# A two-block transformer on one core: weight splits ordered behind the layer norm at stage borders, the mean in one instruction, first loads and last columns cut differently

## The chip, the cores and the metric

The kernel runs on one core of one Trainium2 chip. The metric is the device time of one execution in microseconds (us). Runs of this kernel lie between 2589.7 and 2595.17 us, so a change of less than 0.2% (5.2 us) can hardly be told from none.

## The reference, cut to what matters

256 tokens of width 1024 pass through two blocks of two layers each, all in float32. The stages that the change touches are these:

```python
# first block, for l in 0, 1
x = layer_norm(a*x + 0.5*swiglu(x, ffn1_w1[l], ffn1_w3[l], ffn1_w2[l]), ln1_g[l], ln1_b[l])
x = layer_norm(a*x + token_mixing(x, w_in[l], ...), ln2_g[l], ln2_b[l])
x = layer_norm(a*x + cross_attention(x, mem, ...), ln3_g[l], ln3_b[l])
x = layer_norm(a*x + 0.5*swiglu(x, ffn2_w1[l], ffn2_w3[l], ffn2_w2[l]), ln4_g[l], ln4_b[l])
# second block, for l in 0, 1
x = x + 0.5*swiglu(rmsnorm(x), ...); x = x + mixer_l(rmsnorm(x)); x = x + 0.5*swiglu(rmsnorm(x), ...)
x = x + sigmoid(rmsnorm(x) @ ple_gate[l]) * (p[l] @ ple_proj[l])
return rmsnorm(x, final_norm)
```

Here `swiglu(h, w1, w3, w2) = (silu(h @ w1) * (h @ w3)) @ w2`, with w1 and w3 of 1024 x 2816 and w2 of 2816 x 1024.

## The kernel before

The 256 tokens are two tiles of 128 rows, called t = 0 and t = 1. Every matrix product takes each operand as a sum of two parts, hi + lo, and adds three matmuls (`mm3`): x_hi w_hi, x_hi w_lo and x_lo w_hi, lines 191, 192 and 193. TensorE (PE) runs these; a stationary tile is 128 x 128 of x, and up to 512 columns of w stream past it.

**Weights.** A `slot` is a piece of a weight matrix of 128 x 1024 elements (two k blocks of 512 columns, or one k block of 1024). It is loaded by SyncE (SP) into one of four `raw` buffers; then ScalarE (ACT) copies each half into `whi` (line 177) and VectorE (DVE) subtracts to get `wlo` (line 178). Eight pairs of `whi` and `wlo` exist. A raw buffer is free for the next load when its two copies and two subtractions are done; loads are issued in one order on SP's queue.

**A stage's border.** A stage ends in `lin_rows`: t = 0 finishes first, its layer norm runs beside the matmuls of t = 1, then comes t = 1. The layer norm (`layer_norm`) forms y and its row sums on DVE (`lny`, line 344), the mean in two DVE instructions (347, 348), the square sum on ACT (`lnj`, 351), 1/sigma on DVE and GpSimd (353, 354, a power), then the normalized row on DVE (358, 359). `x_to_T` turns it with eight PE transposes, and ACT and DVE split the result into `xT` (304, 305; 386, 387 where a row scale is folded in). The turn of t = 1 is put off as `pend`.

The next stage begins with `lin_first`. It runs all its weight slots (four for each of its one or two `specs`) for t = 0 alone; after a number of matmuls given by its argument `at`, `flush` issues the put-off turn of t = 1; then it runs the same slots for t = 1. So 48 matmuls on t = 0 hide the layer norm of t = 1 where there are two specs. The slots are numbered here in the order in which they are made, 0 to 7.

The order on each engine is fixed when the program is made, by a planner that takes instructions by their place in the program and by its own idea of when their inputs are ready; `issue_after(ins)` makes the planner put an instruction after `ins` if both are on the same engine, without a wait on the chip.

**The ends.** At the start x of t = 0 is loaded whole, then two slots of w1, then x of t = 1, then the two broadcast rows `G` and `B` of the first layer norm (512 KB each), then more slots. At the end the last stage (`ple_step` with no next norm) forms for each 512-column half a sigmoid, a product, a sum and a square sum, then 1/rms, then for each half one DVE instruction and one store.

Of the kernel before, what the change touches and what calls it, by code (L numbers as in the profile page):

```python
# [11 lines left out]
ALU = mybir.AluOpType  # L12
# [82 lines left out]
class Core:  # L95
    def __init__(self, tc, ctx, a):
        self.tc, self.a = tc, a
        nc = self.nc = tc.nc
        self.V, self.A, self.G, self.T = nc.vector, nc.scalar, nc.gpsimd, nc.tensor
        e = ctx.enter_context  # L100

        self.wsp = e(tc.tile_pool(name="wsp", bufs=8))
        self.xp = e(tc.tile_pool(name="xp", bufs=1))
        self.bp = e(tc.tile_pool(name="bp", bufs=11))
        self.cst = e(tc.tile_pool(name="cst", bufs=1))
        self.wraw = e(tc.tile_pool(name="wraw", bufs=4))
        self.rp = e(tc.tile_pool(name="rp", bufs=2))
        self.gbp = e(tc.tile_pool(name="gbp", bufs=1))
        self.sc2 = e(tc.tile_pool(name="sc2", bufs=7))
        self.sc4 = e(tc.tile_pool(name="sc4", bufs=2))  # L110
        self.biasp = e(tc.tile_pool(name="biasp", bufs=2))
        self.smp = e(tc.tile_pool(name="smp", bufs=5))
        self.accp = e(tc.tile_pool(name="accp", bufs=4, space=PSUM))
        self.atp = e(tc.tile_pool(name="atp", bufs=2, space=PSUM))
        self.tpp = e(tc.tile_pool(name="tpp", bufs=2, space=PSUM))
        self.pend = None
        self.ident = self.const("c_ident")
        self.mhalf = self.cst.tile([P, 32], F32, name="mhalf")
        self.V.memset(self.mhalf, -0.5)
        self.one = self.cst.tile([P, 1], F32, name="one")  # L120
        self.V.memset(self.one, 1.0)
# [97 lines left out]
    def lin_first(self, X, specs, at):  # L219


        ps = [[self.bank("lin") for _ in specs] for _ in range(2)]
        slots, i = [], 0
        for t in range(2):
            for j, (wv, c0, n, evac) in enumerate(specs):
                for b in range(4):
                    if t == 0:
                        slots.append(wv(b) if callable(wv) else self.slot_kn(wv, 2 * b, 2, c0, n))
                    wh, wl = slots[4 * j + b]
                    for k in range(2):  # L230
# [24 lines left out]
    def lin_rows(self, X, ks, wv, done, skew=6, mid=None, last=False, late=None):  # L255

        o = [[self.bank("o") for _ in range(2)] for _ in range(2)]
        ks = list(ks)  # L260
# [3 lines left out]
        def unit(w, kk, t, hs=(0, 1)):  # L264
            xh, xl = X(kk, t)
            for h in hs:
                sl = slice(h * 512, h * 512 + 512)
# [21 lines left out]
        with self.tc.issue_after(mm.ins):  # L289
            if last:  # L290
                todo = [(w, kk, (h,)) for h in range(2) for w, kk in ws]
# [46 lines left out]
    def layer_norm(self, t, x, o, c, G, B, xT):  # L338
# [8 lines left out]
        self.V.tensor_add(mu[:, 0:1], sm[:, 0:1], sm[:, 1:2])  # L347
        self.V.tensor_scalar_mul(mu[:, 1:2], mu[:, 0:1], -1.0 / D)
        var = self.sm(1, "var")
        junk = self.s4(name="lnj")  # L350
        self.A.activation(junk, y, AF.Square, bias=mu[:, 1:2], accum_out=var)
# [4 lines left out]
        for h in range(2):  # L356
            sl = slice(h * 512, h * 512 + 512)
            self.V.scalar_tensor_tensor(xn[:, sl], y[:, sl], mu[:, 1:2], G[:, sl], op0=ALU.add, op1=ALU.mult)
            self.V.scalar_tensor_tensor(xn[:, sl], xn[:, sl], rs, B[:, sl], op0=ALU.mult, op1=ALU.add)
# [46 lines left out]
    def ffn(self, xT, w1, w3, w2, done, rs=None, mid=None, pre=()):  # L406
# [18 lines left out]

        for c in range(5):
            if c == 0:
                h = [[None, None], [None, None]]

# [4 lines left out]
                yield from self.lin_first(X, [(first(w1v), 0, 512, keep(0)), (first(w3v), 0, 512, keep(1))], 36)  # L434
            else:
                h = [[self.bank("h") for _ in range(2)] for _ in range(2)]
            for i, wv in enumerate((w1v, w3v) if c else ()):
                for k0 in range(0, 8, 2):
# [5 lines left out]
                    if i == 0 and k0 == 0:  # L444
# [382 lines left out]
    def mixing(self, l, xT, done):  # L827
# [14 lines left out]
        def plain(c0, n, dst):  # L842
# [17 lines left out]
                               38))  # L860
# [654 lines left out]
def body(tc, a):  # L1515
    with ExitStack() as ctx:
# [5 lines left out]
        pre = []  # L1522
        for t in range(2):
            if t == 1:
                pre = [k.slot_kn(w1v, 2 * i, 2, 0, 512) for i in range(2)]
            x[t] = k.new_x(t)
            nc.sync.dma_start(out=x[t], in_=a["x"][0, t * P:(t + 1) * P, :])
            for h in range(2):
                tp = k.tp()
                for j in range(4):  # L1530
                    k.T.transpose(tp[:, j, :], x[t][:, (4 * h + j) * P:(4 * h + j + 1) * P], k.ident)
                k.split_to(xT[:, 4 * h:4 * h + 4, 0, t * P:(t + 1) * P],
                           xT[:, 4 * h:4 * h + 4, 1, t * P:(t + 1) * P], tp)
# [4 lines left out]
        def ln_step(g, b, c, norm=None):  # L1538

            G = k.row_bcast(g, "G")  # L1540
            B = k.row_bcast(b, "B")
            gcol = k.rows_T([rows(norm)], "gcol") if norm is not None else None
            st = {}

            def done(t, o):
                if t == 0:
                    st["T"] = k.new_xT()
                x[t], fin = k.layer_norm(t, x[t], o, c, G, B, st["T"])
# [26 lines left out]
        def ple_step(norm):  # L1575
# [5 lines left out]
            def done(t, o):  # L1581
# [5 lines left out]
                def part(h):  # L1587
                    sl = slice(h * 512, h * 512 + 512)
                    k.A.activation(s[:, sl], o[h], AF.Sigmoid, scale=rs[t])
# [3 lines left out]
                if norm is not None:  # L1593
                    for h in range(2):
                        part(h)
# [4 lines left out]
                else:  # L1600
                    ss = k.sm(2, "fss")
                    for h in range(2):
                        part(h)
                        k.mean_sq(ss[:, h:h + 1], xn[:, h * 512:h * 512 + 512], 512)
                    r = k.sm(1, "frs")
                    k.V.tensor_add(r, ss[:, 0:1], ss[:, 1:2])
                    k.V.tensor_scalar(r, r, 0.5, RMS_EPS, op0=ALU.mult, op1=ALU.add)
                    k.G.tensor_tensor(r, r, k.mhalf[:, 0:1], op=ALU.pow)
                    for h in range(2):
                        sl = slice(h * 512, h * 512 + 512)  # L1610
                        k.V.scalar_tensor_tensor(s[:, sl], xn[:, sl], r, G[:, sl], op0=ALU.mult, op1=ALU.mult)
# [5 lines left out]
        for l in range(2):  # L1617
            st, done = ln_step(a["ln1_g"][l], a["ln1_b"][l], 0.5)
            run_all(k.ffn(xT, a["ffn1_w1"][l], a["ffn1_w3"][l], a["ffn1_w2"][l], done, pre=pre,
                          mid=lambda: k.mixing_prep(l)))  # L1620
            pre = []
            xT = st["T"]
            st, done = ln_step(a["ln2_g"][l], a["ln2_b"][l], 0.5)
            memT = k.mixing(l, xT, done)
            xT = st["T"]
            st, done = ln_step(a["ln3_g"][l], a["ln3_b"][l], 1.0)
            k.xattn(l, xT, memT, done)
            xT = st["T"]
            st, done = ln_step(a["ln4_g"][l], a["ln4_b"][l], 0.5, a["ffn_norm_2"][0, 0] if l == 1 else None)
            run_all(k.ffn(xT, a["ffn2_w1"][l], a["ffn2_w3"][l], a["ffn2_w2"][l], done))  # L1630
# [53 lines left out]
```

## Time and profile before

| | us |
|---|---|
| median of 3 runs (2589.7 to 2595.17) | 2589.87 |
| the profiled execution, its own time | 2592.86 |
| its span, first to last instruction | 2590.9 |
| PE busy | 2557.8 (99%) |
| DVE busy | 1654.6 (64%) |
| ACT busy | 1405.3 (54%) |

PE, DVE, ACT, POOL and SP are TensorE, VectorE, ScalarE, GpSimd and SyncE; PEld is PE's weight load. The page gives each engine's busy time. Matmuls are pipelined, so the time from the start of one to the start of the next is less than the duration that a row shows. A view of waits names the instruction that waited, and after the arrow the engine and instruction that ended its wait. A view of stretches lists for each engine the busy time and in brackets the instructions that overlap the stretch, in the order PE, PEld, DVE, ACT, POOL.

### The profile page before, as it was taken

The numbers are of one execution on the slowest core, as the hardware profiler recorded it, in microseconds if no ns is written. First come the engines' busy times: TensorE is split into PE (matmuls) and PEld (weight loads), VectorE is DVE, ScalarE is ACT, GpSimd is POOL, SyncE is SP. The second block draws the span as 40 slices with busy tenths as digits, with TensorE's granted clock in tenths as the row PEclk, the third lists the DMA queues.
The fourth block names the chain that finished last, engine by engine and source line by source line (L and its number), as shares of the span: only waits on it lengthen the run. The fifth ranks groups of instructions, "written<-read, shape, count | busy, mean of one in ns | idle before, by whom it ended". The sixth has DMA issues, their size and how long they took to land.

```text
span 2590.9 us, 35713 instructions
## 1 busy us (share of the span) xinstructions
PE 2557.8 (99%) x12769; PEld 2136.5 (82%) x12769; DVE 1654.6 (64%) x3254; ACT 1405.3 (54%) x2804; POOL 78.1 (3%) x122
## 2 busy tenths in 40 slices
PE   8999999999999999999999999999999999999998
PEld 7888888888888889878888888887788788878887
DVE  6548687676556557687775565567655655566555
ACT  5445646555545445546555455456644645766544
POOL 0000010000000000010000000000000000000000
PEclk9999999999999999999999999999999999999999
DMA  8658655547556558564456556563665665454652
GB/s 282 189 163 229 185 163 158 162 147 219 183 177 211 189 163 228 166 177 139 156 180 201 188 180 196 188 178 111 192 188 182 194 187 194 140 171 148 195 190 98
DMA packets 261800, 465.40 MB, mean 180 GB/s; under 512 B 25963, under 2 KB 96119, under 8 KB 261623
## 3 DMA queue, kind: packets, MB, share of 16 engines
q1 hardware_dynamic: 261622, 463.13, 58.4%
q8 instruction: 100, 1.64, 0.3%
q14 instruction: 78, 0.63, 0.1%
HBM read 462.02 MB, written 1.05 MB: 179 GB/s over the span
## 4 chain that ended last, share of the span: by engine, by line
PE 91%; DVE 4%; ACT 2%; DMA 2%; issue 1%; POOL 0%; DVEq 0%; POOLq 0%; SPq 0%; ACTq 0%
PE h L193 9%; PE h L191 9%; PE h L192 9%; PE lin L193 8%; PE lin L191 8%; PE lin L192 8%; PE o L193 8%; PE o L192 8%; PE o L191 8%; PE tp L313 2%; PE linT L251 2%; PE linT L250 2%; PE linT L249 2%; DVE wlo L178 1%; PE po L542 1%; PE ht L193 1%
## 5 line engine op out<-in xcount | busy, mean ns | idle before, releaser
L178 DVE TENSOR_TENSOR wlo<-raw,whi 128x512 fp32r<-128x512 f32 (+2 forms) x1682 | 1095.3, 687 | 650.6 <-ACT whi L177 646.4
L177 ACT CAST whi<-raw 128x512 fp32r<-128x512 f32 (+2 forms) x1682 | 962.5, 615 | 813.7 <-PE h L193 313.5
L191 PE MATMUL h<-whi,xT 128*128 128x512 f32 x1024 | 401.2, 392 | 0.0
L193 PE MATMUL h<-whi,xT 128*128 128x512 f32 x1024 | 398.9, 390 | 0.0
L192 PE MATMUL h<-wlo,xT 128*128 128x512 f32 x1024 | 398.7, 389 | 0.0
L191 PE MATMUL lin<-whi,xT 128*128 128x512 f32 (+1 forms) x912 | 363.0, 400 | 4.2 <-ACT xT L386 2.1
L193 PE MATMUL lin<-whi,xT 128*128 128x512 f32 (+1 forms) x912 | 353.0, 390 | 3.2 <-DVE xT L305 3.2
L192 PE MATMUL lin<-wlo,xT 128*128 128x512 f32 (+1 forms) x912 | 353.1, 388 | 0.2 <-DVE wlo L178 0.2
L191 PE MATMUL o<-whi,gT 128*128 128x512 f32 x704 | 276.1, 392 | 0.0
L192 PE MATMUL o<-wlo,gT 128*128 128x512 f32 x704 | 274.9, 391 | 0.0
L193 PE MATMUL o<-whi,gT 128*128 128x512 f32 x704 | 274.1, 389 | 0.0
L193 PEld LDWEIGHTS h<-whi,xT 128*128 128x128 f32 x1024 | 192.2, 188 | 40.1
L192 PEld LDWEIGHTS h<-wlo,xT 128*128 128x128 f32 x1024 | 192.4, 188 | 39.1
L191 PEld LDWEIGHTS h<-whi,xT 128*128 128x128 f32 x1024 | 192.3, 188 | 38.8
L191 PEld LDWEIGHTS lin<-whi,xT 128*128 128x128 f32 x912 | 171.9, 189 | 43.9 <-ACT xT L386 6.6
L193 PEld LDWEIGHTS lin<-whi,xT 128*128 128x128 f32 x912 | 171.7, 188 | 39.8 <-DVE xT L305 4.3
L192 PEld LDWEIGHTS lin<-wlo,xT 128*128 128x128 f32 x912 | 172.2, 189 | 32.0 <-DVE wlo L178 1.0
L193 PEld LDWEIGHTS o<-whi,gT 128*128 128x128 f32 x704 | 132.2, 188 | 27.4
L191 PEld LDWEIGHTS o<-whi,gT 128*128 128x128 f32 x704 | 132.2, 188 | 26.8
L192 PEld LDWEIGHTS o<-wlo,gT 128*128 128x128 f32 x704 | 132.3, 188 | 26.3
L249 PE MATMUL linT<-xT,whi 128*128 128x256 f32 (+1 forms) x264 | 75.2, 285 | 0.0
L251 PE MATMUL linT<-xT,wlo 128*128 128x256 f32 (+1 forms) x264 | 74.9, 284 | 0.0
(474 smaller groups left out, 3163.8 us busy)
## 6 DMA issues: line engine op xcount, KB each, us to landing
raw<-in_ffn_w SPq DMA_DIRECT2D x496, 512.0 KB
raw<-in_w_in SPq DMA_DIRECT2D x120, 512.0 KB
raw<-in_m_w_in SPq DMA_DIRECT2D x52, 512.0 KB
raw<-in_ffn_w SPq DMA_DIRECT2D x64, 256.0 KB
raw<-in_w_o SPq DMA_DIRECT2D x16, 512.0 KB
raw<-in_m_w_out SPq DMA_DIRECT2D x16, 512.0 KB
raw<-in_ple_gate SPq DMA_DIRECT2D x16, 512.0 KB
bias<-in_b_in SPq DMA_DIRECT2D x24, 256.0 KB
```

The costliest lines, as they stand in the source:

```text
L177: self.A.copy(hi[:, v], raw[:, v])
L178: self.V.tensor_sub(lo[:, v], raw[:, v], hi[:, v].bitcast(F32))
L191: mm(ps, xh, wh, start=start, stop=False)
L192: mm(ps, xh, wl, start=False, stop=False)
L193: return mm(ps, xl, wh, start=False, stop=stop)
L249: mm(ps[:m, :], wh[:, k, :], xh, start=(k == 0), stop=False)
L250: mm(ps[:m, :], wh[:, k, :], xl, start=False, stop=False)
L251: mm(ps[:m, :], wl[:, k, :], xh, start=False, stop=(k == nk - 1))
L313: self.T.transpose(tp[:, j, :], src[:, (b + j) * P:(b + j + 1) * P], self.ident)
L542: self.T.matmul(po[:, j * dv:(j + 1) * dv], pT[:, j * (t + 1) + k, :], v_of(hs[j], k), start=(k == 0), stop=(k == t))
```

## The change

It has five parts.

1. `layer_norm` takes the mean in one DVE instruction instead of two and remembers three of its instructions in `heads`: the mean, the square, the last of line 359. The next `lin_first` puts slots 3 and 4 behind the square (on ACT) and the mean (on DVE), and slots 5 to 7 behind the square and the last of line 359. `heads` is that of t = 1.
2. `at` becomes 32 for the feed-forward stages (from 36) and 35 for the mixing stage (from 38).
3. At the start x of t = 0 comes in two halves with the first slot's two halves between them, x of t = 1 comes after the second slot, its turn becomes `pend`, the first `lin_first` takes w1 alone and `at` 15, and w3 follows in the ordinary loop.
4. `G` and `B` of a layer norm that ends a feed-forward stage are loaded in the middle of that stage's `lin_rows` and no longer ahead of the stage.
5. In the last stage the second half of t = 1 becomes two pieces of 256 columns; the product with the final gain moves ahead of 1/rms; the last scaling is one DVE instruction and one ACT instruction.

```diff
@@ lin_first
+        norm, self.heads = self.heads, None
+
+        def slot(wv, b, c0, n):
+            with ExitStack() as q:
+                if norm is not None and len(slots) >= 3:
+                    q.enter_context(self.tc.issue_after(norm[1].ins))
+                    q.enter_context(self.tc.issue_after(norm[2 if len(slots) >= 5 else 0].ins))
+                return wv(b) if callable(wv) else self.slot_kn(wv, 2 * b, 2, c0, n)
...
-                        slots.append(wv(b) if callable(wv) else self.slot_kn(wv, 2 * b, 2, c0, n))
+                        slots.append(slot(wv, b, c0, n))
@@ lin_rows
+        cols = [[(0, 512), (512, 512)] for _ in range(2)]
         o = [[self.bank("o") for _ in range(2)] for _ in range(2)]
+        if last:
+            cols[1][1:] = [(512, 256), (768, 256)]
+            o[1] = [o[1][0], o[1][1][:, 0:256], self.at("o")[:, 0:256]]
...
-                todo = [(w, kk, (h,)) for h in range(2) for w, kk in ws]
+                todo = [(w, kk, (h,)) for h in range(3) for w, kk in ws]
@@ layer_norm
-        self.V.tensor_add(mu[:, 0:1], sm[:, 0:1], sm[:, 1:2])
-        self.V.tensor_scalar_mul(mu[:, 1:2], mu[:, 0:1], -1.0 / D)
+        m = self.V.tensor_scalar(mu[:, 1:2], sm[:, 0:1], sm[:, 1:2], -1.0 / D, op0=ALU.add, op1=ALU.mult)
...
-        self.A.activation(junk, y, AF.Square, bias=mu[:, 1:2], accum_out=var)
+        sq = self.A.activation(junk, y, AF.Square, bias=mu[:, 1:2], accum_out=var)
...
-            self.V.scalar_tensor_tensor(xn[:, sl], xn[:, sl], rs, B[:, sl], op0=ALU.mult, op1=ALU.add)
+            v = self.V.scalar_tensor_tensor(xn[:, sl], xn[:, sl], rs, B[:, sl], op0=ALU.mult, op1=ALU.add)
+        self.heads = (m, sq, v)
@@ ffn
+        start = bool(pre)
...
-                yield from self.lin_first(X, [(first(w1v), 0, 512, keep(0)), (first(w3v), 0, 512, keep(1))], 36)
+                specs = [(first(w1v), 0, 512, keep(0)), (first(w3v), 0, 512, keep(1))]
+                yield from self.lin_first(X, specs[:1] if start else specs, 15 if start else 32)
...
-            for i, wv in enumerate((w1v, w3v) if c else ()):
+            for i, wv in enumerate((w1v, w3v)):
+                if h[0][i] is not None:
+                    continue
@@ mixing
-                               38))
+                               35))
@@ body
+        x = [k.new_x(t) for t in range(2)]
+        def load_x(t, h):
+            sl = slice(h * 512, h * 512 + 512)
+            nc.sync.dma_start(out=x[t][:, sl], in_=a["x"][0, t * P:(t + 1) * P, sl])
+
+        def first_parts(raw):
+            v = raw.rearrange("p (k n) -> p k n", n=512)
+            yield v[:, 0:1], w1v[:, 0:1, 0:512]
+            load_x(0, 1)
+            yield v[:, 1:2], w1v[:, 1:2, 0:512]
+        load_x(0, 0)
+        pre = [[w.rearrange("p (k n) -> p k n", n=512) for w in k.slot(first_parts, 1024)]]
+        k.x_to_T(0, x[0], xT)
+        pre.append(k.slot_kn(w1v, 2, 2, 0, 512))
+        for h in range(2):
+            load_x(1, h)
+        k.pend = lambda: k.x_to_T(1, x[1], xT)
@@ ple_step, no next norm
+                    for i, ps in enumerate(o):
+                        n = ps.shape[-1]
+                        part(ps, slice(c0, c0 + n))
+                        junk = k.s2(name="junk")
+                        k.A.activation(junk[:, :n], xn[:, c0:c0 + n], AF.Square, scale=512.0 ** -0.5,
+                                       accum_out=ss[:, i:i + 1])
+                        k.V.tensor_mul(s[:, c0:c0 + n], xn[:, c0:c0 + n], G[:, c0:c0 + n])
+                        c0 += n
                     r = k.sm(1, "frs")
                     k.V.tensor_add(r, ss[:, 0:1], ss[:, 1:2])
+                    if t == 1:
+                        k.V.tensor_add(r, r, ss[:, 2:3])
                     k.V.tensor_scalar(r, r, 0.5, RMS_EPS, op0=ALU.mult, op1=ALU.add)
                     k.G.tensor_tensor(r, r, k.mhalf[:, 0:1], op=ALU.pow)
+                    k.V.tensor_scalar_mul(s[:, 0:512], s[:, 0:512], r)
+                    k.A.mul(s[:, 512:1024], s[:, 512:1024], r)
                     for h in range(2):
                         sl = slice(h * 512, h * 512 + 512)
-                        k.V.scalar_tensor_tensor(s[:, sl], xn[:, sl], r, G[:, sl], op0=ALU.mult, op1=ALU.mult)
                         nc.sync.dma_start(out=a["out"][0, t * P:(t + 1) * P, sl], in_=s[:, sl])
@@ body, the loop over the layers (the loads of G and B are now a function, load)
             run_all(k.ffn(xT, a["ffn1_w1"][l], a["ffn1_w3"][l], a["ffn1_w2"][l], done, pre=pre,
-                          mid=lambda: k.mixing_prep(l)))
+                          mid=lambda: (st["load"](), k.mixing_prep(l))))
...
-            run_all(k.ffn(xT, a["ffn2_w1"][l], a["ffn2_w3"][l], a["ffn2_w2"][l], done))
+            run_all(k.ffn(xT, a["ffn2_w1"][l], a["ffn2_w3"][l], a["ffn2_w2"][l], done, mid=st["load"]))
```

## Rows read from the trace of the kernel before

**Rows 1.** The page: span, busy time of two engines, the chain by engine.
```profile
span 2590.9 us, 35713 instructions
PE 2557.8 (99%) x12769; PEld 2136.5 (82%) x12769; DVE 1654.6 (64%) x3254; ACT 1405.3 (54%) x2804; POOL 78.1 (3%) x122
...
PE 91%; DVE 4%; ACT 2%; DMA 2%; issue 1%; POOL 0%; DVEq 0%; POOLq 0%; SPq 0%; ACTq 0%
```

**Rows 2.** Waits of PE, whole span: releaser, us in total, times, longest.
```profile
PE tp L1531 <- DMA x<-in_x: 5.5, 1, 5.5
...
PE lin L193 <- DVE xT L305: 3.2, 3, 1.3
...
PE tp L326 <- DVE xT L387: 0.9, 1, 0.9
PE tp L369 <- DVE x L359: 0.7, 1, 0.7
...
PE tp L326 <- DVE xT L305: 0.5, 1, 0.5
```

**Rows 3.** Stretches, start: us, busy time by engine (count), clock, DMA share, GB/s.
```profile
3.00:9.00 6.00, 2.31 (x9) 1.85 (x9) 1.60 (x3) 2.12 (x5) 0.00 (x0) 1.00 1.02 397
9.00:16.00 7.00, 6.67 (x24) 4.89 (x24) 5.05 (x9) 4.30 (x9) 0.00 (x0) 1.00 1.02 363
...
0.00:30.00 30.00, 22.71 (x90) 17.44 (x91) 17.42 (x31) 17.85 (x30) 0.50 (x5) 1.00 0.87 296
```

**Rows 4.** Timeline of ACT, start: start us, us, instruction, [idle before, releaser].
```profile
13.79 1.14 ACT L177 CAST whi<-raw 128x512 fp32r<-128x512 f32 x2 [1.79 <-DMA raw<-in_ffn_w]
15.14 1.14 ACT L177 CAST whi<-raw 128x512 fp32r<-128x512 f32 x2 [0.22 <-DMA raw<-in_ffn_w]
```

**Rows 5.** The chain that ended last, start: start us, us, what.
```profile
1.17 4.18 DMA x<-in_x
```

**Rows 6.** Timeline of PE, 20 us: two of one block's three products.
```profile
20.44 0.40 PE L193 MATMUL lin<-whi,xT 128*128 128x512 f32 x1
20.84 0.50 PE L192 MATMUL lin<-wlo,xT 128*128 128x512 f32 x1
```

**Rows 7.** Stretches of PE alone: 512-column, then 256-column matmuls.
```profile
2572.00:2580.00 8.00, 8.00 (x37) 1.00 0.02 6
534.00:538.00 4.00, 4.00 (x36) 1.00 0.94 303
```

**Rows 8.** Timeline of all engines, end of the kernel.
```profile
2582.37 0.69 ACT L1589 ACTIVATE sgate<-o,rs 128x512 f32<-128x512 f32 x1 [0.65 <-PE o L193]
...
2586.31 1.41 DVE L1611 SCALAR_TENSOR_TENSOR sgate<-x,frs,G 128x512 f32<-128x512 f32 x2 [0.66 <-POOL frs L1608]
2587.09 1.00 SPq L1612 DMA_DIRECT2D out<-sgate  x2
```

**Rows 9.** Timeline of ACT, 208 us: a 256-column square.
```profile
208.42 0.42 ACT L375 ACTIVATE junk<-zl 128x256 f32<-128x256 f32 x1 [3.19 <-DVE zl L840]
```

**Rows 10.** Timeline of DVE, border into the second layer's first feed-forward stage.
```profile
760.90 1.42 DVE L359 SCALAR_TENSOR_TENSOR x<-x,rs,B 128x512 f32<-128x512 f32 x2 [0.66 <-POOL rs L354]
...
765.84 1.28 DVE L178 TENSOR_TENSOR wlo<-raw,whi 128x512 fp32r<-128x512 f32 x2
767.04 0.68 DVE L344 SCALAR_TENSOR_TENSOR lny<-x,o 128x512 f32<-128x512 f32 x1
...
768.25 0.69 DVE L178 TENSOR_TENSOR wlo<-raw,whi 128x512 fp32r<-128x512 f32 x1
...
772.97 1.41 DVE L359 SCALAR_TENSOR_TENSOR x<-x,rs,B 128x512 f32<-128x512 f32 x2 [0.44 <-POOL rs L354]
```

**Rows 11.** Timeline of ACT at the same border.
```profile
770.50 1.15 ACT L351 ACTIVATE lnj<-lny,mu 128x1024 f32<-128x1024 f32 x1
```

**Rows 12.** The chain that ended last, border at 1519 us: a weight load.
```profile
1519.68 4.24 DMA raw<-in_ffn_w
```

**Rows 13.** A stretch inside a feed-forward stage, columns as in rows 3.
```profile
130.00:180.00 50.00, 50.00 (x223) 40.77 (x222) 25.27 (x41) 21.87 (x44) 0.00 (x0) 1.00 0.57 178
```

More of the change, by code (lines that the diff above doesn't have):

```diff
@@ L116, in __init__ @@
         self.pend = None
+        self.heads = None
         self.ident = self.const("c_ident")
@@ L262, in lin_rows, with unit @@
         units = [0]
-        def unit(w, kk, t, hs=(0, 1)):
+        def unit(w, kk, t, hs=None):
             xh, xl = X(kk, t)
-            for h in hs:
-                sl = slice(h * 512, h * 512 + 512)
+            for h in hs or range(len(cols[t])):
+                sl = slice(cols[t][h][0], sum(cols[t][h]))
                 mm = self.mm3(o[t][h], xh, xl, w[0][:, 0, sl], w[1][:, 0, sl], kk == ks[0], kk == ks[-1])
@@ L424, in first @@
             return lambda b: pre.pop(0) if pre else self.slot_kn(wv, 2 * b, 2, 0, 512)
+        start = bool(pre)
         for c in range(5):
+            h = [[None, None], [None, None]]
             if c == 0:
-                h = [[None, None], [None, None]]
                 def keep(i):
@@ L433, in keep @@
                     return f
-                yield from self.lin_first(X, [(first(w1v), 0, 512, keep(0)), (first(w3v), 0, 512, keep(1))], 36)
-            else:
-                h = [[self.bank("h") for _ in range(2)] for _ in range(2)]
-            for i, wv in enumerate((w1v, w3v) if c else ()):
+                specs = [(first(w1v), 0, 512, keep(0)), (first(w3v), 0, 512, keep(1))]
[3 more added lines that the diff above has]
+                    continue
+                for t in range(2):
+                    h[t][i] = self.bank("h")
                 for k0 in range(0, 8, 2):
@@ L443, in ffn @@
                             mm = self.mm3(h[t][i], xh, xl, wh[:, k, :], wl[:, k, :], k0 + k == 0, k0 + k == 7)
-                    if i == 0 and k0 == 0:
+                    if c and i == 0 and k0 == 0:
                         with self.tc.issue_after(mm.ins):
@@ L1521, in body @@
         w1v = a["ffn1_w1"][0].rearrange("(k p) c -> p k c", p=P)
[L1522 to L1533, printed above, removed]
+        x = [k.new_x(t) for t in range(2)]
[14 more added lines that the diff above has]
+        k.pend = lambda: k.x_to_T(1, x[1], xT)
         rs = [None, None]
@@ L1538, in ln_step, with load @@
         def ln_step(g, b, c, norm=None):
-            G = k.row_bcast(g, "G")
-            B = k.row_bcast(b, "B")
+            st = {}
+            def load():
+                st["G"] = k.row_bcast(g, "G")
+                st["B"] = k.row_bcast(b, "B")
             gcol = k.rows_T([rows(norm)], "gcol") if norm is not None else None
-            st = {}
+            st["load"] = load
             def done(t, o):
@@ L1547, in done @@
                     st["T"] = k.new_xT()
-                x[t], fin = k.layer_norm(t, x[t], o, c, G, B, st["T"])
+                x[t], fin = k.layer_norm(t, x[t], o, c, st["G"], st["B"], st["T"])
                 if norm is None:
@@ L1585, in done, with part @@
                 s = k.s4(name="sgate")
-                def part(h):
-                    sl = slice(h * 512, h * 512 + 512)
-                    k.A.activation(s[:, sl], o[h], AF.Sigmoid, scale=rs[t])
+                def part(ps, sl):
+                    k.A.activation(s[:, sl], ps, AF.Sigmoid, scale=rs[t])
                     k.V.tensor_mul(s[:, sl], s[:, sl], k.pp[t][:, sl])
@@ L1594, in done @@
                     for h in range(2):
-                        part(h)
+                        part(o[h], slice(h * 512, h * 512 + 512))
                     rs[t] = k.row_scale(t, xn)
@@ L1600, in done @@
                 else:
[L1601 to L1604, printed above, removed]
+                    ss = k.sm(4, "fss")
+                    c0 = 0
+                    for i, ps in enumerate(o):
[6 more added lines that the diff above has]
+                        c0 += n
                     r = k.sm(1, "frs")
                     k.V.tensor_add(r, ss[:, 0:1], ss[:, 1:2])
+                    if t == 1:
+                        k.V.tensor_add(r, r, ss[:, 2:3])
                     k.V.tensor_scalar(r, r, 0.5, RMS_EPS, op0=ALU.mult, op1=ALU.add)
                     k.G.tensor_tensor(r, r, k.mhalf[:, 0:1], op=ALU.pow)
+                    k.V.tensor_scalar_mul(s[:, 0:512], s[:, 0:512], r)
+                    k.A.mul(s[:, 512:1024], s[:, 512:1024], r)
                     for h in range(2):
                         sl = slice(h * 512, h * 512 + 512)
-                        k.V.scalar_tensor_tensor(s[:, sl], xn[:, sl], r, G[:, sl], op0=ALU.mult, op1=ALU.mult)
                         nc.sync.dma_start(out=a["out"][0, t * P:(t + 1) * P, sl], in_=s[:, sl])
@@ L1623, in body @@
             st, done = ln_step(a["ln2_g"][l], a["ln2_b"][l], 0.5)
+            st["load"]()
             memT = k.mixing(l, xT, done)
@@ L1626, in body @@
             st, done = ln_step(a["ln3_g"][l], a["ln3_b"][l], 1.0)
+            st["load"]()
             k.xattn(l, xT, memT, done)
```

## The prediction, made before the changed kernel ran

> **What bounds the kernel now.** I read the page first: PE is busy for 2557.8 of 2590.9 us, and 91% of the chain that ended last is PE [rows 1]. No edit here takes matmuls away, so what can be won is only time in which PE stands still or runs slowly. The view of PE's waits says where that is: 5.5 us before the first transpose, for the load of x; and four lines at stage borders, together 3.2 + 0.9 + 0.7 + 0.5 = 5.3 us, in which PE waits for an xT or x of a layer norm [rows 2]. Then the stretches of the start and the timeline of the end show the two tails. So three places, each small: the start, the end, the borders.
>
> Two spacings serve below. 37 matmuls of 512 columns overlap a stretch of 8.00 us [rows 7], and one lasts 0.40 [rows 6], so they start every (8.00 + 0.40)/37 = 0.227 us. 36 of 256 columns overlap 4.00 us, which gives about 0.119. A transpose (128 columns) I put at 0.11, below the second.
>
> **The start.** 90 PE instructions overlap the first 30 us [rows 3]: 16 transposes and 74 matmuls, worth 74 x 0.227 + 16 x 0.11 = 18.6 us. PE has lost 11.4 us by then. The reason is loads: from 3 to 16 us the DMA engines are full (share 1.02) at 397 and then 363 GB/s, and ACT idles for the landing of slot 2 (13.79) and stands ready for slot 3 (15.14) [rows 3, 4]. Ahead of slot 2 in the queue stand the identity, x (two tiles), slots 0 and 1, and G and B; the change takes G and B, 1.05 MB, out of there. At 363 to 397 GB/s they cost 2.6 to 2.9 us, so slot 2 lands near 11.0 and slot 3 near 12.4. Its two copies take 1.14 [rows 4], its second subtraction 0.69 [rows 10], two products 0.45: the pass over t = 0, which is w1 alone now, ends near 14.7. Done by then: 24 x 0.227 + 16 x 0.11 = 7.2, lost 7.5. After that no load is short: the pass over t = 1 needs no new slot for 24 x 0.227 = 5.4 us, in which about four land (0.524 MB at 397 GB/s is 1.3 us each), and w3 is then used for both tiles at 2.7 us a slot. Gain 11.4 - 7.5 = 3.9. Bounds: 2.0 if the splits of x come in the way or PE, with less to do early, is slow for longer; 5.2 if the 1.3 us between slots 2 and 3 vanish too.
>
> That x comes in halves brings forward only the first transposes. The load took 4.18 us [rows 5], and 0.26 MB less at 397 GB/s is 0.7 us earlier; PE then waits for slot 2 anyway, so I count nothing for it. The Trainium skill (DMA: Bandwidth & Descriptors, section Bandwidth) advises the opposite, batches of at least 1 MiB, and gives a fixed cost of about 2.0 us for each transfer, which it measured on another issuing path. By it a half load would take 2.0 + 0.6 = 2.6 us, and the whole 3.2, where the trace has 4.18. Both agree on some 0.6 us for the half, and neither moves the sum.
>
> **G and B in mid stage.** Eight loads of 0.524 MB move into `lin_rows`, where in 50 us PE is never idle and the DMA share is 0.57 [rows 13]. Cost 0; without that cover 1.3 us each. SP's queue at the borders loses two loads that wait there for the old layer norm to let go of the buffers; that hurts nobody behind them.
>
> **The end.** From the last sigmoid to the end of the last scaling it is 2586.31 + 1.41 - 2582.37 = 5.35 us [rows 8]. Four of the steps (sigmoid, product, sum, square) shrink from 512 to 256 columns: the sigmoid takes 0.69, an ACT instruction of 256 columns 0.42 [rows 8, 9]. So 0.27 each, 1.1 together (0 if the cost is all fixed, 1.4 if it halves). An addition more costs 0.2. The two final instructions, 1.41 in a row, become one on DVE beside one on ACT, 0.7 at most: gain 0.7. The second store must still follow the first on SP, whose two issues take 1.00 [rows 8]; that gives back 0.2. PE pays 24 matmuls of 512 columns made into 48 of 256: 24 x (2 x 0.119 - 0.227) = 0.26. Sum 1.1 - 0.2 + 0.7 - 0.2 - 0.26 = 1.1; bounds 0.3 and 1.6. For the last term the Trainium skill (TensorE: Matmul & The Clock Gate, Back-to-back issue gap) gives 262 cycles at 256 columns and 518 at 512. By it the price would be 24 x 6 cycles, 0.06 us, and the end 0.2 us better; the trace's spacings are larger and are taken.
>
> **The borders.** The cleanest one to cost is that into the second layer's first feed-forward stage, where PE waits for nothing today. y of t = 1 begins at 767.04 and ends at 768.25, but a split's subtraction takes DVE there [rows 10], two more follow between the two instructions of the mean, and the square starts only at 770.50 [rows 11]. Line 359 starts at 772.97, 2.47 after the square, and ends at 774.38 [rows 10].
> With the change no split of slots 3 to 7 may go there. The mean follows y; between nothing and 0.68 (a whole row of y) I take 0.3 for one single-column instruction. Square at 768.55, line 359 at 771.0, end at 772.4: the layer norm is 2.0 us earlier, here for nothing, at the borders with waits for up to the 5.3 us.
> The price: slots 3 and 4, which are split before y today, now come behind the square. ACT's copies start at 768.55 + 1.15 = 769.7 and take 0.57 a half; slot 3's second half is copied at 770.8. Its subtraction finds DVE busy with line 359 until 772.4 and ends at 773.0, if the planner puts line 359 first. PE comes to need it at 767.0 + (18 + 3 + 1) x 0.227 = 772.0. So PE can wait 1.0 us there, and 1.4 if the first half also comes behind line 359. On the other side, PE's order is not rigid: where a wlo was late, the planner put line 193 ahead of line 192 [rows 6], and two products of three need whi alone; then next to nothing is left.
> A second check is DVE's whole load from y to the end of the pass: y 1.2, mean 0.3, lines 358 and 359 2 x 1.41, ten subtractions at 1.28 - 0.69 = 0.59 to 0.69 each, xT 1.28 like two subtractions: 11.5 to 12.5 us, against 48 x 0.227 + 8 x 0.11 = 11.8 on PE. So it is full, and 0 to 0.7 late. Between 0 and 1.4 I take 0.6 at each of six borders (two into mixing, four into feed-forward): 3.6 in place of 5.3, gain 1.7; bounds +5.3 and 5.3 - 8.4 = -3.1. The two borders into cross attention have one spec, and the value projection ahead of it; slot 3 is late there for nobody: 0.
> The smaller `at` starts the turn of t = 1 one block, 0.7 us, earlier, less than the 2.0 by which x is earlier: 0. At the three feed-forward stages with no layer norm ahead I also take 0, since the scale is not waited for there (0.7 each at worst).
>
> **Sum.** 3.9 + 1.1 + 1.7 = 6.7 us of the profiled execution's 2592.86, which is 3.0 above the median of the runs; on the median 2589.87 - 6.7 = 2583.2.
>
> **Rivals.**
> 1. Borders clear. The planner orders products by whi first, nothing waits: 3.9 + 1.1 + 5.3 = 10.3, to 2579.6. For: the 2.0 us by which each layer norm ends earlier covers the longest border wait, 1.3 [rows 2]. Against: DVE's full 11.8 us.
> 2. The reordering does nothing on balance. Splits made late cost PE what the layer norm saved, 1.0 us at each of six borders: 3.9 + 1.1 - 0.7 = 4.3, to 2585.6. For: slot 3 is needed before line 359 ends. Against: rows 6.
> 3. The start is not held by loads but by splits and a slow PE; only 2.0 come: 2.0 + 1.1 + 1.7 = 4.8, to 2585.1. For: from 3 to 9 us PE runs only 9 instructions in 2.31 us of busy time [rows 3]. Against: the DMA share of 1.02.
> 4. Slower: slot 7's load. It takes slot 3's raw buffer, which becomes free only at 773.0 instead of ahead of y. A weight load at a border took 4.24 [rows 12]: landed at 777.2, copied and subtracted by 778.5, needed at 767.0 + 42 x 0.227 + 0.9 = 777.4. At 4.24 that is 1.1 us, of which 0.6 is in my sum. The kernel gets slower by 0.2% once six borders lose (5.0 + 5.3 + 5.2)/6 = 2.6 us each, that is with a load of 5.7 us or more: 2595.1 and up. For: loads there run beside G, B and biases in the mixing stage. Against: at the feed-forward borders G and B are gone.
>
> **How the numbers follow.** My forecast 0.42 (from -5.3 to -9), rival 1 0.14, rival 2 0.23, rival 3 0.12, rival 4 0.09. 0.2%, 5.2 us, is about what a measurement of this kernel can tell from no change. More than that faster: rival 1 and nearly all of the forecast, 0.54; within it: rivals 2 and 3 and the rest, 0.38; slower 0.08. The range adds the bounds: best 5.2 + 1.6 + 5.3 = 12.1, to 2577.8; worst 2.0 + 0.3 - 3.1 = -0.8, to 2590.7. The likeliest case's own range is 2581 to 2584.6.
>
> **What the profile after would show.** Right: ACT's copy of slot 2 near 11 us and the last t = 0 matmul of w1 near 14.7; about 3.7 us from the last sigmoid to the last scaling; at each border one mean instruction right behind y, the square within 0.5 us of it, and no split between. PE's waits for xT at borders give way to shorter waits for wlo at line 192. Wrong: PE waits of over 1 us for wlo of slot 3 or for a raw load of slot 7, a start in which slot 2 still lands after 13, or a border whose layer norm ends no earlier because ACT or DVE is held by something else, such as the turn of t = 0.

## The result: slower by 0.6%, outside the range

The changed kernel takes 2607.0 us (median of 6 runs, 2601.6 to 2610.55) beside 2591.78 for the kernel before (6 runs, 2589.7 to 2595.17): a ratio of 1.0057, 95% interval 1.0044 to 1.0070. The forecast was 2583.2, with a range of 2577.8 to 2590.7. Its profiled execution took 2605.54, 12.7 us above the 2592.86 of the one before.

The page after, beside [rows 1]: PE is busy 8 us more, with 24 matmuls more (those of the end that were cut in two).

```profile
span 2603.7 us, 35739 instructions
PE 2565.6 (99%) x12793; PEld 2137.3 (82%) x12793; DVE 1657.9 (64%) x3244; ACT 1406.8 (54%) x2809; POOL 82.7 (3%) x122
```

PE's waits after, columns as in [rows 2]. The small waits for xT and x of [rows 2] are gone; in their place stand waits for wlo and whi of the weights, and two of 2.4 us on average for an xT.

```profile
PE lin L193 <- DVE wlo L179: 6.3, 12, 0.9
...
PE lin L192 <- ACT xT L319: 4.8, 2, 2.5
...
PE lin L192 <- ACT whi L178: 2.3, 7, 0.6
```

**Where the time went.** I set the start of each matmul beside that of the same matmul in the kernel before, and call the difference the shift. At 125 us it is -1.2: the start gained. Then it jumps at each of the eight layer-norm borders (the second and sixth lead into cross attention, the first and fifth into mixing), in their order by +2.1, +2.0, +2.1, +2.3, +1.2, +2.8, +1.4 and +0.3, together +14.2, and it hardly moves elsewhere (+0.4 over the second block). The end gives back 0.6. -1.2 + 14.2 + 0.4 - 0.6 = 12.8, the growth of the span.

**One border, line by line**: the one of [rows 10, 11]. The chain that ended last (start, us, what) runs from y (lny) through the layer norm, two subtractions and a weight load back to PE:

```profile
771.06 1.39 DVE lny L359 x4
...
776.23 1.30 DVE wlo L179 x2
777.54 5.43 DMA raw<-in_ffn_w
783.00 0.63 ACT whi L178
...
784.40 0.50 PE lin L193
```

The timelines of DVE, ACT and PE there. All eight subtractions of slots 3 to 6 come in one row after line 373 (359 before); PE waits at 776.97 for slot 3's wlo and at 784.40 for slot 7's.

```profile
774.90 1.41 DVE L373 SCALAR_TENSOR_TENSOR x<-x,rs,B 128x512 f32<-128x512 f32 x2 [0.66 <-POOL rs L368]
776.23 4.90 DVE L179 TENSOR_TENSOR wlo<-raw,whi 128x512 fp32r<-128x512 f32 x8
```
```profile
772.80 1.16 ACT L365 ACTIVATE lnj<-lny,mu 128x1024 f32<-128x1024 f32 x1 [3.84 <-DVE mu L362]
...
773.96 4.25 ACT L178 CAST whi<-raw 128x512 fp32r<-128x512 f32 x8
...
783.00 1.14 ACT L178 CAST whi<-raw 128x512 fp32r<-128x512 f32 x2 [1.15 <-DMA raw<-in_ffn_w]
```
```profile
775.62 0.62 PE L192 MATMUL lin<-whi,xT 128*128 128x512 f32 x2
776.97 0.50 PE L193 MATMUL lin<-wlo,xT 128*128 128x512 f32 x1 [0.73 <-DVE wlo L179]
777.31 0.39 PE L194 MATMUL lin<-whi,xT 128*128 128x512 f32 x1
...
782.85 0.39 PE L194 MATMUL lin<-whi,xT 128*128 128x512 f32 x1
783.67 0.50 PE L192 MATMUL lin<-whi,xT 128*128 128x512 f32 x1 [0.43 <-ACT whi L178]
784.40 0.50 PE L193 MATMUL lin<-wlo,xT 128*128 128x512 f32 x1 [0.22 <-DVE wlo L179]
```

Against a spacing of 0.227, the first wait costs 777.31 - 775.62 - 3 x 0.227 = 1.0 us; the second 1.2, counted in the same way from 782.85 to 784.74, the next start after the last row.

This is SP's queue at the border. G and B of the next layer norm are issued as the old one lets go of their buffers (lines 372 and 373 end at 774.13 and 776.31); slot 7's raw load comes behind them, at the moment at which slot 3's second subtraction (the end of the 1.30 us above) frees its buffer.

```profile
774.16 0.34 SPq L166 DMA_DIRECT2D G<-in_ln_g  x1
776.34 0.34 SPq L166 DMA_DIRECT2D B<-in_ln_b  x1
777.54 12.03 SPq L175 DMA_DIRECT2D raw<-in_ffn_w  x6
```

### The profile page after: what moved, and what is told of

It is laid out like the page before. It is cut to its first block, busy times and chain, and to the rows that moved or that the text cites. A ratio compares the mean times of both kernels' runs of the same rounds, so it can differ in the third digit from the quotient of the medians.

```text
span 2603.7 us, 35739 instructions
## 1 busy us (share of the span) xinstructions
PE 2565.6 (99%) x12793; PEld 2137.3 (82%) x12793; DVE 1657.9 (64%) x3244; ACT 1406.8 (54%) x2809; POOL 82.7 (3%) x122
## 4 chain that ended last, share of the span: by engine, by line
PE 88%; DVE 5%; DMA 3%; ACT 2%; issue 1%; POOL 0%; SPq 0%; POOLq 0%; ACTq 0%; DVEq 0%
PE h L194 9%; PE h L193 9%; PE h L192 9%; PE o L194 8%; PE o L193 8%; PE o L192 8%; PE lin L192 7%; PE lin L194 7%; PE lin L193 7%; DVE wlo L179 2%; PE tp L328 2%; DMA raw<-in_ffn_w 2%; PE linT L261 2%; PE linT L260 2%; PE linT L259 2%
## 5 line engine op out<-in xcount | busy, mean ns | idle before, releaser
L192 PE MATMUL h<-whi,xT 128*128 128x512 f32 x1040 | 407.4, 392 | 0.0
L194 PE MATMUL h<-whi,xT 128*128 128x512 f32 x1040 | 405.1, 389 | 0.0
L193 PE MATMUL h<-wlo,xT 128*128 128x512 f32 x1040 | 404.9, 389 | 0.0
L192 PE MATMUL lin<-whi,xT 128*128 128x512 f32 (+1 forms) x896 | 358.6, 402 | 9.7 <-ACT xT L319 4.8
L194 PE MATMUL lin<-whi,xT 128*128 128x512 f32 (+1 forms) x896 | 348.6, 391 | 0.0
L194 PEld LDWEIGHTS h<-whi,xT 128*128 128x128 f32 x1040 | 195.2, 188 | 40.7
L192 PEld LDWEIGHTS h<-whi,xT 128*128 128x128 f32 x1040 | 195.3, 188 | 39.6
```

Of the source, the lines that this page charges most:

```text
L192: mm(ps, xh, wh, start=start, stop=False)
L193: mm(ps, xh, wl, start=False, stop=False)
L194: return mm(ps, xl, wh, start=False, stop=stop)
```

## The experiments

Queueing is the name used here for part 1 of the change, the splits put behind the layer norm. Theory A: the queueing alone loses the borders. It splits into the lateness of slot 3's own wlo, and a weight load that starts late and meets G and B. Rival B: G and B in mid stage, `at` or the mean disturb the borders. All 12 runs in one table: the median, the ratio to the kernel before with its interval, and the shift of the profiled execution in three parts: at 125 us (start), from there to 1560 us (eight borders), from there to the last matmul.

| run | us | ratio (95%) | start | borders | rest |
|---|---|---|---|---|---|
| the change | 2607.0 | 1.0057 (1.0044-1.0070) | -1.2 | +14.2 | +0.4 |
| e1 no queueing | 2588.3 | 0.9987 (0.9978-0.9996) | -2.2 | -4.9 | +4.9 |
| e2 before + queueing | 2608.49 | 1.0058 (1.0045-1.0072) | 0.0 | +15.3 | +1.1 |
| e3 G, B behind raw | 2593.69 | 1.0005 (0.9996-1.0014) | -1.5 | +2.8 | -0.3 |
| e4 before + start | 2588.52 | 0.9990 (0.9981-0.9999) | -1.5 | -0.9 | +1.8 |
| e5 G, B of 64 columns | 2595.32 | 1.0011 (1.0003-1.0020) | -1.5 | +3.2 | +4.8 |
| e6 queueing from slot 5 | 2586.87 | 0.9980 (0.9971-0.9989) | -1.7 | -6.1 | +2.6 |
| e7 e1 + x whole | 2587.54 | 0.9982 (0.9974-0.9991) | -1.5 | -2.8 | +0.4 |
| e8 e1 + sigmoid first | 2586.48 | 0.9981 (0.9972-0.9990) | -1.6 | -4.7 | +1.0 |
| e9 e6 + sigmoid first | 2585.08 | 0.9976 (0.9967-0.9985) | -1.5 | -6.2 | -0.9 |
| e10 queueing from slot 4 | 2588.41 | 0.9991 (0.9982-0.9999) | -2.1 | -4.1 | +0.7 |
| e11 e9, old `at` | 2586.0 | 0.9980 (0.9971-0.9989) | -1.5 | -5.2 | +2.7 |
| e12 e9, x whole, early matmuls | 2588.5 | 0.9986 (0.9977-0.9994) | -2.9 | -6.3 | +3.8 |

The last column is mostly TensorE's clock (last section), so small differences are read from the other two, and with care. In the change, e2 and e4 the borders hold stretches at the lower clock too, worth 1.7, 3.4 and 1.7 us. And e1, e7 and e8, whose code at the borders is the same, read -4.9, -2.8 and -4.7. A good part of each gain there lies at the fifth border (-2.4, -0.9 and -2.2 in these three), where e4, which keeps the old layer norm, gains 2.3 as well. So a difference of 2 us in that column does not by itself tell two kernels apart.

**e1.** `if norm is not None and len(slots) >= 3:` becomes `if False:`.

> The changed kernel without the queueing: no split is put behind the layer norm; all other parts stay. Theory A (the queueing alone costs the 14 us that the eight borders lost): about 2591.8 - 1.2 (start) - 0.6 (end) = 2590, and less by what the single mean instruction gives; PE waits for no wlo of slot 3 and no raw load of slot 7 at a border. Rival B (the loads of G and B in mid stage, the smaller at or the single mean disturb the borders): 2598 or more, the steps at the borders stay.

2588.3, against 2607.0 with the queueing; nothing is left of the jumps. Rival B is out.

**e2.** The kernel before, with `slot()` of the diff and its three remembered instructions.

> The kernel before with the queueing alone (the mean in two instructions, G and B, at, start and end as they were). Theory A: the borders lose their 14 us here too, 2604 to 2607. Rival B: less than half of that, under 2599.

2608.49. The queueing is the whole loss, with G and B loaded at the old place in the program, too.

**e3.** On SP, G and B behind the raw loads.

```diff
+            with k.tc.issue_after(k.first_raw.ins):   # slot 7's raw load
                 st["G"] = k.row_bcast(g, "G")
                 st["B"] = k.row_bcast(b, "B")
```

(In mixing and cross attention they are loaded after the eighth slot, and after the four slots of the output projection.)

> The changed kernel, and on SP the loads of G and B are put behind the raw loads of the eight first slots (in cross attention behind the four of the output projection), instead of ahead of the eighth. Theory A1 (the late loads come from SP's queue: G and B stand there waiting for the old layer norm, and the raw loads behind them): the waits for slot 7 and for the output projection's weights go, some 1.5 us at six borders and 2.5 at two, so 2593 to 2597. Theory A2 (the raw buffers themselves become free late, since their splits come late): the six borders stay as they are and only the two into cross attention can gain, 2602 to 2607.

2593.69: by its time A1, 13.3 us regained. But the trace shows another way. SP and ACT at the border:

```profile
772.42 6.74 SPq L176 DMA_DIRECT2D raw<-in_ffn_w  x5
```
```profile
767.68 1.15 ACT L377 ACTIVATE lnj<-lny,mu 128x1024 f32<-128x1024 f32 x1 [3.84 <-DVE mu L374]
...
776.62 1.15 ACT L179 CAST whi<-raw 128x512 fp32r<-128x512 f32 x2
```

Slot 7's load is issued 772.42 - 767.68 = 4.74 us after the square; in the changed kernel it is 777.54 - 772.80 = 4.74 as well. So SP did not hold it; the late buffer did, as A2 says. What changed is the load: copied 4.2 us after its issue without a wait for it, in place of 5.5 with one. PE's waits for wlo stay (5.4 us, 8 times, against 6.3). So A1 had the time and A2 the reason for the late issue; neither had named the shorter load.

**e5.** The same order, fewer bytes: `k.load_bcast(st[nm][:, 0:64], row[0:64])`, and lines 372 and 373 read these 64 columns sixteen times. The kernel leaves out the other columns of G and B.

> The changed kernel with its order on SP, but the layer norms' G and B loads cut from 1024 to 64 columns, which are used for all columns (work left out: the other columns of G and B). Theory D (the eighth slot's load is late because the bytes of G and B run ahead of it in the DMA engines): the time from its issue to ACT's copy falls from 5.5 us to about 4.2, as in the run with G and B behind it, six borders gain 1.3 us each, about 2599. Theory S (it is late because SP is held): its issue moves or nothing changes, 2605 to 2608. By both the borders into cross attention stay, where three weight loads are issued only after B.

SP and ACT there:

```profile
769.24 0.34 SPq L166 DMA_DIRECT2D G<-in_ln_g  x1
771.41 0.34 SPq L166 DMA_DIRECT2D B<-in_ln_b  x1
772.62 6.72 SPq L175 DMA_DIRECT2D raw<-in_ffn_w  x5
```
```profile
767.88 1.15 ACT L365 ACTIVATE lnj<-lny,mu 128x1024 f32<-128x1024 f32 x1 [3.85 <-DVE mu L362]
...
776.80 1.15 ACT L178 CAST whi<-raw 128x512 fp32r<-128x512 f32 x2
```

Again issued 4.74 after the square, behind G and B as before, and copied 4.2 later: theory D. The bytes of G and B, not their place on SP, made the load late. 2595.32 is better than D's 2599, since I had been wrong on the borders into cross attention. There, too, the issue stays (in the changed kernel 540.83, 4.74 after the square at 536.09; here 538.72, 4.74 after 533.98) and the load shortens: 546.34 - 540.83 = 5.5 becomes 542.41 - 538.72 = 3.7. SP, ACT and PE there in the changed kernel, where the copy stands ahead of xT on ACT; then SP and ACT of e5:

```profile
540.83 2.74 SPq L175 DMA_DIRECT2D raw<-in_xattn_wo  x3
546.34 1.14 ACT L178 CAST whi<-raw 128x512 fp32r<-128x512 f32 x2 [4.30 <-DMA raw<-in_xattn_wo]
...
547.86 1.07 ACT L319 CAST xT<-tp 128x512 fp32r<-128x512 f32 x2
548.50 0.50 PE L192 MATMUL lin<-whi,xT 128*128 128x512 f32 x1 [2.48 <-ACT xT L319]
```
```profile
538.72 2.73 SPq L175 DMA_DIRECT2D raw<-in_xattn_wo  x3
542.41 1.14 ACT L178 CAST whi<-raw 128x512 fp32r<-128x512 f32 x2 [2.48 <-DMA raw<-in_xattn_wo]
```

The changed kernel holds a check of its own: at the eighth border a single row (G of the final norm) stands ahead of slot 7's load, which is issued at 1541.84 and copied at 1545.69, 3.85 later, and PE does not wait for it; the jump there is only 0.3.

**e6, e10.** `len(slots) >= 5` and `>= 4` in place of `>= 3`.

> The changed kernel with the queueing for slots 5 to 7 alone; slots 3 and 4 are split where the planner likes. With this the raw load of the eighth slot stands ahead of G and B on SP again. If late splits of slot 3 cost the 0.9 us that PE waits at a border, and its late buffer the rest: all 14 us come back, 2586 to 2589, at best below the 2588.3 without queueing since DVE's layer norm stays earlier. If the queueing of slots 5 to 7 hurts too: 2592 or more.

> The changed kernel with the queueing from slot 4 on; slot 3 alone is free. If slot 3 is the whole price (its own late wlo, 0.9 us at six borders, and the raw buffer that slot 7 takes from it): as with queueing from slot 5, 2586 to 2589. If every slot that comes late costs (slot 4's wlo is needed 1.4 us after slot 3's): 2590 or more, with a wait for a wlo at each border.

2586.87: with slots 3 and 4 free nothing is lost. Whether the queueing of slots 5 to 7 gains anything is not shown: the borders read 6.1 us of gain (6.2 and 6.3 in e9 and e12, which queue alike) against 2.8 to 4.9 with no queueing, but the medians' intervals overlap (e1 0.9978-0.9996, e6 0.9971-0.9989). From slot 4 on it is 2588.41 and 4.1, with 1.5 us of waits for wlo in four places (0.2 us in one place in e6). So slot 3 is nearly the whole price; slot 4 costs about 2 us at most.

**e4, e7, e12: the start.** e4 is the kernel before with part 3 of the change, and G and B in mid stage. e7 is e1 with x and slot 0 each in one load. e12 is e9 with that start and eight matmuls ahead of the first transpose:

```diff
+        z = k.s2(name="zz"); k.V.memset(z, 0.0)
+        for i in range(2):
+            zp = k.tp()
+            for j in range(4):
+                k.T.matmul(zp[:, j, :], z[:, 0:P], z[:, 0:P], start=True, stop=True)
```

> The kernel before with the change's start alone and G and B in mid stage (no queueing, old mean, old at beyond the first stage, old end). If the start gives what the changed kernel's trace shows at 125 us, 1.2 us: about 2590.6, and slot 2 is copied at 12.3. If it gives the 3.9 us of the forecast, and the changed kernel lost it again to something else before 125 us: about 2588, slot 2 near 11.0. If G and B in mid stage cost something at the borders: above 2592.

> The changed kernel without the queueing (2588.3), with x and the first slot each loaded in one piece again; order, one spec and at 15 stay. If the halves are why slot 2 is copied at 11.6 to 12.3 us in place of the forecast 11.0 (two more transfers, shorter rows, a lower rate): copy near 11, the shift at 125 us grows from 2.2 to about 3, time 2587.5. If only the bytes ahead of it count: slot 2 as late as there, the first product some 0.9 us later, time 2588 to 2589.

> The run with slot 5 and the sigmoid, with x and slot 0 in one piece each, and eight matmuls of 128 columns on zeros ahead of the first transpose (work added, results unused). With x whole the loads came at 10.9 and 12.2 us and yet nothing was won at 125 us: the first 15 products were spaced 0.43 us, the later ones 0.23. If they are slow because PE did nothing before: spaced 0.23 from the first one on or soon after, a shift of -3 to -4 us at 125 us in place of -1.5. If not, or if the idle stretch behind the eight undoes it: 0.43 again until about 12.4, and no shift.

e4's median, 2588.52, is that of its second case, but its trace is that of the first: slot 2 is copied at 12.28 and the start gains 1.5. What else it gains is not in the start; the fifth border gives 2.3.

ACT's copies of slot 2 in the changed kernel, and of slots 2 and 3 in e7:

```profile
12.26 1.14 ACT L178 CAST whi<-raw 128x512 fp32r<-128x512 f32 x2 [1.56 <-DMA raw<-in_ffn_w]
```
```profile
10.88 1.14 ACT L178 CAST whi<-raw 128x512 fp32r<-128x512 f32 x2 [1.32 <-DMA raw<-in_ffn_w]
12.24 1.15 ACT L178 CAST whi<-raw 128x512 fp32r<-128x512 f32 x2 [0.22 <-DMA raw<-in_ffn_w]
```

Stretches, the same two kernels (columns as in [rows 3]): 320 GB/s with halves, 389 without. In the first of these stretches the ten runs with halves read 298 to 320, and e12, the other run without, 378.

```profile
3.00:9.00 6.00, 3.76 (x12) 2.85 (x13) 2.30 (x4) 2.21 (x4) 0.00 (x0) 1.00 0.94 320
```
```profile
3.00:9.00 6.00, 3.36 (x11) 2.38 (x12) 1.97 (x4) 2.59 (x6) 0.00 (x0) 1.00 1.02 389
9.00:12.00 3.00, 3.00 (x9) 2.32 (x8) 2.19 (x4) 1.68 (x4) 0.00 (x0) 1.00 1.03 374
```

So with whole loads slots 2 and 3 land at 10.9 and 12.2, and still only 1.5 us come out, no more than in the runs with halves (1.2 to 2.2), where 3 had been expected. PE, never idle from 9 to 12 us, runs its products at nearly twice the spacing until 12.4 (e7's PE):

```profile
11.53 0.63 PE L194 MATMUL lin<-whi,xT 128*128 128x512 f32 x1
11.96 0.63 PE L192 MATMUL lin<-whi,xT 128*128 128x512 f32 x1
12.38 0.53 PE L193 MATMUL lin<-wlo,xT 128*128 128x512 f32 x1
12.74 0.39 PE L194 MATMUL lin<-whi,xT 128*128 128x512 f32 x1
12.97 0.39 PE L192 MATMUL lin<-whi,xT 128*128 128x512 f32 x1
```

In e12 they are spaced 0.23 from 8.30 on, apart from waits, and the start gains 2.9: the slow spacing was what held the start of e7. Its median, 2588.5, is nevertheless above e9's: in the profiled execution its last column is worse by 4.7 us, of which two stretches at the lower clock near 2290 and 2300 us take 3.4; e9 has none there. Whether the early matmuls have a part in that is open.

**e8, e9: the end.** The square and the gain product of the piece before move behind the last piece's sigmoid and sum (`held` is that piece).

```diff
+                        sg, ad = part(ps, slice(c0, c0 + n))
+                        if held:
+                            with ExitStack() as q:
+                                q.enter_context(k.tc.issue_after(sg.ins))
+                                q.enter_context(k.tc.issue_after(ad.ins))
+                                rest(*held)
```

> The changed kernel without the queueing (2588.3), and at the end the last piece's sigmoid, product and sum go ahead of the square of the piece before. If the end gained 0.55 us in place of the forecast 1.1 because the last sigmoid stands on ACT behind that square (it starts 0.90 us after the last matmul, before 0.03): it starts within 0.1 us of the last matmul and the end is 0.6 to 0.9 us shorter, time 2587.5. If not: no shorter.

> The two edits that gained, together: queueing from slot 5 on (2586.9 alone) and the last sigmoid ahead of the square (0.7 us at the end). If they add, 2586 and below, faster than the kernel before by 0.2%; PE waits for no slot 3 and no slot 7 at the borders, and the chain from the last matmul to the last scaling is 4.3 us or less.

ACT at the end, the changed kernel and then e8. The last matmul ends at 2595.70 in the one and 2576.99 in the other (started at 2595.42 and 2576.71, 0.28 long).

```profile
2596.18 0.42 ACT L1633 ACTIVATE junk<-x 128x256 f32<-128x256 f32 x1 [0.95 <-DVE x L1617]
...
2596.60 0.46 ACT L1615 ACTIVATE sgate<-o,rs 128x256 f32<-128x256 f32 x1
...
2599.56 0.72 ACT L1644 ACTIVATE sgate<-sgate,frs 128x512 f32<-128x512 f32 x1 [1.04 <-POOL frs L1642]
```
```profile
2577.02 0.48 ACT L1615 ACTIVATE sgate<-o,rs 128x256 f32<-128x256 f32 x1 [0.50 <-PE o L194]
...
2580.27 0.72 ACT L1658 ACTIVATE sgate<-sgate,frs 128x512 f32<-128x512 f32 x1 [1.31 <-POOL frs L1656]
```

From the last matmul to the end of the last scaling: 4.58 us, then 4.00; before 5.38. So the sigmoid starts 0.03 after the last matmul, as expected, and the end is 0.6 shorter, the least of the 0.6 to 0.9 expected. e9, with both edits, has the lowest median of the study: 2585.08, faster than the one before by 0.24% (0.15 to 0.33). Its expectation held: PE waits for no weight at the eight borders, and the end takes 4.00 as in e8.

**e11.** e9 with `at` 36 and 38.

> The run with slot 5 and the sigmoid, with the old values of at (36 and 38) beyond the first stage. Forecast: the smaller at is worth nothing, within 1 us of that run. Rival: the turn of t = 1, one block later, is what hides the layer norm; then 0.7 us a border less wait, up to 5 us faster, or as much slower where the next stage waits for it.

2586.0, within 1 us, and the intervals overlap. In the trace the old values lose 1.0 us over the eight borders, 0.5 at each border into mixing; by the spread above that is too little to call it a price.

## Why the prediction was wrong, step by step

**Borders: forecast a gain of 1.7, measured a loss of 14.2.** The layer norm did end earlier, as worked out: from the start of y to the end of the last instruction of line 373 it takes 5.25 us (771.06 to 776.31), before 7.34 [rows 10], so 2.1 against the 2.0 said. It was the price that failed, in three places. Times of the two kernels are compared by way of the stage's first product, which PE starts at 766.49 before and at 771.54 after, 5.05 later.

- *Slot 3's wlo*: taken at 0.6, bounds 0 to 1.4; it is 1.0 at this border. The subtraction came behind line 373 for the first half as well, the dearer of the two cases named. That the size is near is partly luck: the sum let the products start at 767.0, where the trace before has 766.49, so slot 3 is needed 0.5 earlier than said; and the layer norm ended at 776.31 - 5.05 = 771.3, where 772.4 was said, since y began 1.0 earlier too.
- *Slot 7's load*: the step that failed is "SP's queue at the borders loses two loads that wait there for the old layer norm to let go of the buffers; that hurts nobody behind them", and with it the line against rival 4, "at the feed-forward borders G and B are gone". Moved in the program, they were not moved on SP: the planner put them where they first could run, directly ahead of slot 7. The buffer came free as I had said (forecast 773.0; measured 777.54 - 5.05 = 772.5), but I gave the load 4.24 us, and it took 5.43. PE loses 1.2.
- *The two borders into cross attention*, set to 0 since "slot 3 is late there for nobody". Slot 3's raw buffer is needed there too, by the second load of the output projection, whose copy ACT has ahead of xT: PE waits 2.5 and 2.3 us.

As an estimate from the one border shown: six at 1.0 + 1.2 and two at 2.4 are 18.0 gross; 5.3 of the old waits [rows 2] are gone: 12.7. A slower clock behind the sixth border takes 1.7 more (5 us at 0.66, last section), which makes 14.4 beside 14.2. It fits better than its parts: slot 7's load costs half as much at the seventh border and nothing at the eighth, while slot 3's wait is dearer at some others, and the fifth border's old waits also go in e4 without the new layer norm. What the loads behind G and B cost is better read from e3 and e5. Free of that slow stretch, the change loses 12.5 at the borders and they lose 2.8 and 3.2: some 9.5 us are the bytes ahead of slot 7 and of the output projection, and the 3 that stay are slot 3's wlo less the old waits.

So rival 4, given 0.09, had the direction and one of the three mechanisms, the late buffer with a slow load behind it. Its 5.7 us were not needed, since slot 3's own wait and cross attention lost as well and the start brought less.

The Trainium skill (DMA: Bandwidth & Descriptors, section Queues, rings and completion order) says that each DMA engine takes descriptors in the order of its ring. e5 agrees: with G and B still ahead but small, the same load takes 4.2 us or less.

**The start: 3.9, measured 1.2** (1.5 to 2.2 in the other runs with the same start), below even the lower bound of 2.0. The term that failed is the spacing: the sum gave the first products 0.227 us each, and they took 0.427 until about 12 us. The slow PE stood in the bounds and in rival 3; e7 has the forecast's landings and gains 1.5, e12 has quick products as well and gains 2.9. Halves were counted at nothing and made slot 2 late: 12.26 against 10.88, where 11.0 had been forecast. But with PE that slow the lateness cost nothing that shows at 125 us; what halves would cost beside quick products was not run. The Trainium skill (DMA: Bandwidth & Descriptors, section Bandwidth) advises loads of at least 1 MiB, and I had set that aside; 320 GB/s with loads of 256 KB among those of 512 KB, against 389 without, goes the way it says. Which of it is the shorter rows and which the number of transfers isn't told apart here.

**The end: 1.1, measured 0.6.** The 0.26 for PE's 24 more matmuls falls ahead of the last matmul, in the +0.4, so 1.4 is the forecast to set beside 0.6. From the last sigmoid on it is 3.68, the 3.7 of the forecast. Left out was that ACT does the square of the piece before first: the sigmoid starts 0.90 after the last matmul, 0.03 before. With that mended, e8 gains 1.1 from the last matmul to the end of the span.

**`at`**: forecast 0; nothing else is shown (e11). **G and B in mid stage**: free in themselves, as said (e1 and e4 lose nothing), but only because nothing was late behind them.

## What to carry to other kernels

A rule that delays a split delays also the buffer that it reads: follow each late instruction to the next load of that buffer and to what that load meets in the DMA engines (here 5.4 us in place of 4.2), and follow it at every border, including those where the late data itself is in no hurry. Where a planner orders the queues, a load that is moved in the program has not moved until the issue order says so. Delay only what has slack: from slot 5 on the same rule cost nothing, from slot 3 on it cost 0.6%.

## What was not expected of the hardware

- PE at the start (e7): 0.427 us from one 512-column matmul to the next until 12.4 us, which is 512 columns at the lower of the two clock levels (1.2 GHz), while the profile's granted clock for 9 to 12 us is 1.00. Eight early matmuls (e12) brought 0.23 from 8.30 on. The granted clock that the profile shows does not tell of such a start; the spacing does.
- Later the granted clock falls for some microseconds in places that differ between executions. In the changed kernel it fell just after PE had waited 2.3 us at the sixth border (the first row: 5 us at 0.66). In e1 it fell near 2287 us, after a wait of 1.7 (the second row: 0.54); in e9 at the same place, after waits of 1.3 and 1.4, it did not fall. What decides it is open.

```profile
1312.00:1317.00 5.00, 5.00 (x21) 4.13 (x20) 1.84 (x3) 1.95 (x4) 0.00 (x0) 0.66 0.37 112
```
```profile
2287.00:2294.00 7.00, 5.54 (x12) 3.33 (x11) 5.56 (x10) 5.08 (x10) 0.00 (x0) 0.54 0.74 239
```
```profile
2290.00:2305.00 15.00, 15.00 (x94) 12.69 (x93) 6.79 (x13) 9.24 (x15) 0.00 (x0) 1.00 0.42 126
```

The third row is e9's. This is most of the "rest" column, up to 4.9 us in one execution, and why medians a microsecond apart tell little here.
